# Equal groups of 64 rows, and no early store, in a two-way expert dispatch

## The chip, the cores and the metric

The kernel runs on one core of one Trainium2 chip. The metric is the device time in microseconds (us) of that core. Three runs of the kernel before took 239.65, 239.90 and 239.91 us, so the median is 239.9 us.

## The reference

There are 16 x 1024 = 16384 tokens. Each has a vector x of 512 floats and 8 router logits. The softmax of the logits gives eight probabilities, the two largest are kept and divided by their sum, and the token's vector is written out twice, once times each of the two weights:

```python
topk_indices = np.argsort(probs, axis=-1)[..., -k:]            # k = 2
topk_probs = np.take_along_axis(probs, topk_indices, axis=-1)
topk_probs = topk_probs / np.sum(topk_probs, axis=-1, keepdims=True)
x_expanded = x[:, :, np.newaxis, :].repeat(k, axis=2)
return (x_expanded * topk_probs[..., np.newaxis]).astype(np.float32)
```

The smaller of the two weights comes first. In bytes: x is 33.55 MB, the logits are 0.52 MB and the output is 67.11 MB.

## The kernel before, in words

**Layout.** Tokens are dealt to the 128 partitions of the on-chip memory in two groups. In a group of G rows, partition p holds G consecutive tokens; a "row" here is one token in each of the 128 partitions. A row of x is 2 KB in each partition (262,144 bytes in all) and a row of output is 4 KB in each partition (524,288 bytes). The groups have 65 and 63 rows (`GROUPS`, line 42), so in DRAM the pieces of two neighbouring partitions lie 65 or 63 times 2 KB apart in x, and 65 or 63 times 4 KB apart in the output.

**Buffers.** `xs` has room for 65 rows of x. `osp` has room for 18 rows of output, and its first two and a half rows also serve as scratch for the choice of the two largest logits. `WA` holds the two weights of every token.

**Weights.** `top2_weights` (lines 15 to 38) halves the eight logits three times with max and min on VectorE, takes the difference of the two largest and sends it through two sigmoids on ScalarE. Both groups' weights are made at once, after the logits have landed.

**Loads.** `LOADS` (line 44) gives the rows of each load: 6, 28 and 31 in the first group, 4, 28 and 31 in the second. They are issued on SyncE's DMA queue, with the two logits transfers (lines 144 and 145) behind the first. The 4-row load of the second group goes out on ScalarE's queue instead, behind a dummy activation (line 128, `pause`) that waits until the store ahead of the last one has landed. A load into rows of `xs` waits until the store that reads those rows has landed.

**Products and stores.** `STORES` (lines 47 to 50) lists each store: its first row, its number of rows, and where the products are put. "osp" means the buffer `osp` from the given row. "xs" means that the products overwrite rows of `xs` whose x is used up: the tensor-tensor product of line 164 makes 16 rows out of `xs` rows that it writes 32 rows of. Where rows of `osp` are used again, the product is cut in two (`FREE`, line 54): the rows that no store is reading come first, the rest waits until the earlier store has landed. In the first store of the second group, ScalarE makes the last 4 rows (`ACT_ROWS`, line 157), with two activations a row, and VectorE the other 12.

**Order.** Loads and stores are kept in program order on each queue. On SyncE's queue that is: load 6, logits, logits, load 28, load 31, the stores of 15, 16, 15 and 16 rows, load 28, load 31, and the stores of 16, 16, 15 and 16 rows. The first store of all, 3 rows, is issued on ScalarE's queue (line 175).

Of the kernel before, what the change touches and what calls it, by code (L numbers as in the profile page):

```python
# [1 line left out]

# [4 lines left out]

F32 = mybir.dt.float32
ALU = mybir.AluOpType
ACTF = mybir.ActivationFunctionType  # L10
P = 128


def top2_weights(nc, WA, dlt, room, logits, E):

    tt = nc.vector.tensor_tensor
    hi, lo, n = None, None, E  # L20
    while n > 1:
        n //= 2
        if hi is None:
            a, b = logits[:, :, 0:n], logits[:, :, n : 2 * n]
            nhi, nlo = room(n), b
            tt(nhi, a, b, op=ALU.max)  # L26
            tt(nlo, a, b, op=ALU.min)  # L27
        else:
            a, b = hi[:, :, 0:n], hi[:, :, n : 2 * n]
            nhi, nlo, tmp = room(n), room(n), room(n)  # L30
            tt(tmp, lo[:, :, 0:n], lo[:, :, n : 2 * n], op=ALU.max)  # L31
            tt(nlo, a, b, op=ALU.min)  # L32
            tt(nlo, nlo, tmp, op=ALU.max)  # L33
            tt(nhi, a, b, op=ALU.max)  # L34
        hi, lo = nhi, nlo
    tt(dlt, hi[:, :, 0], lo[:, :, 0], op=ALU.subtract)  # L36
    nc.scalar.activation(WA[:, :, 0], dlt, ACTF.Sigmoid, scale=-1.0)  # L37
    nc.scalar.activation(WA[:, :, 1], dlt, ACTF.Sigmoid, scale=1.0)  # L38

GROUPS = [65, 63]

LOADS = [[6, 28, 31], [4, 28, 31]]
BASE = [0, 1]

STORES = [
    [(0, 3, "osp", 0), (3, 15, "osp", 3), (18, 16, "xs", 0), (34, 15, "osp", 0), (49, 16, "xs", 33)],
    [(0, 16, "osp", 2), (16, 16, "xs", 0), (32, 15, "osp", 0), (47, 16, "xs", 32)],
]  # L50

L = 18

FREE = [3, 2]

ACT_ROWS = 4


@with_exitstack
def kernel(  # L60
    ctx: ExitStack,
    tc: tile.TileContext,
    x: bass.AP,
    router_logits: bass.AP,
    k: bass.AP,
    out: bass.AP,
):
    nc = tc.nc
    B, S, D = x.shape
    E = router_logits.shape[-1]  # L70
    N = B * S
    assert int(k) == 2 and E == 8 and N == P * sum(GROUPS)
    M = N // P

    x_v, o_v, rl_v = [], [], []
    t0 = 0
    for n in GROUPS:
        t1 = t0 + P * n
        x_v.append(
            x.rearrange("b s d -> (b s) d")[t0:t1].rearrange("(p m) d -> p m d", p=P)  # L80
        )
        o_v.append(
            out.rearrange("b s k d -> (b s) k d")[t0:t1].rearrange(
                "(p m) k d -> p m k d", p=P
            )
        )
        rl_v.append(
            router_logits.rearrange("b s e -> (b s) e")[t0:t1].rearrange(
                "(p m) e -> p m e", p=P
            )  # L90
        )
        t0 = t1

    wpool = ctx.enter_context(tc.tile_pool(name="wpool", bufs=1))
    xs = wpool.tile([P, max(GROUPS), D], F32)
    osp = wpool.tile([P, L, 2, D], F32)
    WA = wpool.tile([P, M, 2], F32)
    dlt = wpool.tile([P, M], F32)


    flat = osp.rearrange("p l k d -> p (l k d)")
    taken = [0]

    def room(n):
        o = taken[0]
        taken[0] += M * n
        return flat[:, o : o + M * n].rearrange("p (m n) -> p m n", n=n)

    logits = room(E)

    def place(where, at, n):

        if where == "osp":
            return osp[:, at : at + n]
        return xs[:, at : at + 2 * n, :].rearrange("p (r k) d -> p r k d", k=2)

    m0 = 0
    stores = []
    for g, G in enumerate(GROUPS):
        x0, r = BASE[g], 0  # L120
        for n in LOADS[g]:

            late = g == 1 and r == 0
            if late:


                rows = xs[:, x0 : x0 + 2, :]
                pause = nc.scalar.activation(rows, rows, ACTF.Copy)  # L128
                tc.add_manual_dep(
                    pause.ins,  # L130
                    stores[-2].ins.name,
                    mybir.DependencyInfo(
                        mybir.DependencyClass.Sync, mybir.DependencyReason.DATA
                    ),
                    reason="begin when the store ahead of the last has landed",
                )
                tc.keep_in_program_order(pause)
            queue = nc.scalar if late else nc.sync
            load = queue.dma_start(xs[:, x0 + r : x0 + r + n, :], x_v[g][:, r : r + n, :])  # L139
            tc.keep_in_program_order(load)  # L140
            r += n
            if g == 0 and r == 6:
                n0 = GROUPS[0]
                tc.keep_in_program_order(nc.sync.dma_start(logits[:, :n0], rl_v[0]))  # L144
                tc.keep_in_program_order(nc.sync.dma_start(logits[:, n0:], rl_v[1]))  # L145
                top2_weights(nc, WA, dlt, room, logits, E)
        assert r == G
        for r, n, where, at in STORES[g]:
            og = place(where, at, n)

            again = where == "osp" and at == 0 and r > 0
            cuts = [0, FREE[g], n] if again else [0, n]
            if g == 1 and r == 0:
                cuts = [0, n - ACT_ROWS]
                for j in range(n - ACT_ROWS, n):
                    for k2 in range(2):
                        nc.scalar.activation(  # L157
                            og[:, j, k2, :],
                            xs[:, x0 + r + j, :],
                            ACTF.Copy,  # L160
                            scale=WA[:, m0 + r + j, k2 : k2 + 1],
                        )
            for a, b in zip(cuts, cuts[1:]):
                nc.vector.tensor_tensor(  # L164
                    og[:, a:b],
                    xs[:, x0 + r + a : x0 + r + b, :]
                    .unsqueeze(2)
                    .to_broadcast([P, b - a, 2, D]),
                    WA[:, m0 + r + a : m0 + r + b, :]
                    .unsqueeze(3)  # L170
                    .to_broadcast([P, b - a, 2, D]),
                    op=ALU.mult,
                )

            queue = nc.scalar if g == r == 0 else nc.sync
            stores.append(queue.dma_start(o_v[g][:, r : r + n], og))  # L176
            tc.keep_in_program_order(stores[-1])
        m0 += G


# [1 line left out]
_INS = ['x', 'router_logits', 'k']  # L182
_OUTS = [((16, 1024, 2, 512), 'float32')]

_NUMBERS = {'k': 2}


# [26 lines left out]
```

## Time and profile before

| | |
|---|---|
| median of three runs | 239.9 us (239.65 to 239.91) |
| span of the profiled execution | 238.1 us |
| time outside that span, by the median | 1.8 us |
| VectorE busy | 137.6 us, 22 instructions |
| ScalarE busy | 7.9 us, 12 instructions |
| bytes moved by DMA | 101.19 MB, mean 425 GB/s over the span |
| time of the packets on the two DMA queues, as a share of 16 engines' span | 96.1% and 2.6% |

The page gives no time of its own for the profiled execution beside its span, so the median is set beside it. A transfer of 128 partitions is carried out by 16 DMA engines together. "To landing" is the time from the issue of a transfer to the semaphore that tells of its arrival, so it includes the time spent behind earlier transfers of its queue. In the chain of work, which is followed back from the last instruction, such a stretch of waiting is shown as one piece.

### The profile page before, as it was taken

What the parts mean: (1) busy time and instruction counts of PE and PEld (TensorE: products, weight loads), DVE (VectorE), ACT (ScalarE), POOL (GpSimd) and SP (SyncE); (2) the same over time, 40 slices, a digit from 0 to 9 for tenths busy, and PEclk for the clock granted to TensorE, in tenths of its full rate; (3) what the DMA queues carried; (4) which work ended last, traced back from release to release, by engine and by line L of the source; (5) the groups of instructions that cost most, each with busy time, mean ns of one, the idle gap of its engine ahead of it and who ended that gap; (6) DMA issues with size and microseconds to landing.
All of it is one profiled execution on the core that took longest, in us unless ns stands there. A gap on an engine that the chain in (4) does not pass through costs nothing.

```text
span 238.1 us, 115 instructions
## 1 busy us (share of the span) xinstructions
DVE 137.6 (58%) x22; ACT 7.9 (3%) x12; POOL 0.2 (0%) x4
## 2 busy tenths in 40 slices
DVE  0560499999789999100000009999936999950000
ACT  2000000000000000010000007000000000000000
POOL 0000000000000000000000000000000000000000
DMA  7979998979998999989999899898989989979894
GB/s 262 533 337 519 430 418 374 496 341 495 462 396 374 506 433 392 495 352 483 486 396 417 376 479 501 352 506 363 517 363 451 429 363 495 485 341 517 352 528 176
DMA packets 2448, 101.19 MB, mean 425 GB/s; under 512 B 272, under 2 KB 400, under 8 KB 528
## 3 DMA queue, kind: packets, MB, share of 16 engines
q1 hardware_dynamic: 2160, 98.57, 96.1%
q10 hardware_dynamic: 288, 2.62, 2.6%
HBM read 34.08 MB, written 67.11 MB: 425 GB/s over the span
## 4 chain that ended last, share of the span: by engine, by line
DMA 50%; DVE 38%; SPq 1%; issue 0%; DVEq 0%
DMA xs<-in_x_dram 30%; DVE osp L164 24%; DMA out_dram<-osp 20%; DVE xs L164 14%; SPq L144 0%; SPq L145 0%; SPq L139 0%; SPq L176 0%; DVEq L164 0%
## 5 line engine op out<-in xcount | busy, mean ns | idle before, releaser
L164 DVE TENSOR_TENSOR osp<-xs,WA 128x3072 f32<-128x3072 f32 (+4 forms) x7 | 65.1, 9298 | 65.6 <-DMA xs<-in_x_dram 56.8
L164 DVE TENSOR_TENSOR xs<-xs,WA 128x16384 f32<-128x16384 f32 x4 | 68.9, 17225 | 0.2
L157 ACT ACTIVATE osp<-xs,WA 128x512 f32<-128x512 f32 x8 | 5.0, 708 | 37.6 <-DMA xs<-in_x_dram 37.6
L26 DVE TENSOR_TENSOR osp<-osp 128x512 f32<-128x512 f32 x1 | 0.7, 692 | 8.4 <-DMA osp<-in_router_logits_dram 8.4
L128 ACT ACTIVATE xs<-xs 128x1024 f32<-128x1024 f32 x1 | 1.1, 1056 | 90.8 <-DMA out_dram<-osp 90.8
L37 ACT ACT_TABLE_LOAD x1 | 1.3, 1283 | 0.7 <-PEq L195 0.7
L27 DVE TENSOR_TENSOR osp<-osp 128x512 f32<-128x512 f32 x1 | 0.7, 691 | 0.0
L32 DVE TENSOR_TENSOR osp<-osp 128x256 f32<-128x256 f32 (+1 forms) x2 | 0.7, 350 | 0.0
L31 DVE TENSOR_TENSOR osp<-osp 128x256 f32<-128x256 f32 (+1 forms) x2 | 0.7, 350 | 0.0
L33 DVE TENSOR_TENSOR osp<-osp 128x256 f32<-128x256 f32 (+1 forms) x2 | 0.7, 350 | 0.0
L34 DVE TENSOR_TENSOR osp<-osp 128x256 f32<-128x256 f32 (+1 forms) x2 | 0.7, 348 | 0.0
L37 ACT ACTIVATE WA<-dlt 128x128 f32<-128x128 f32 x1 | 0.3, 317 | 10.3 <-DVE dlt L36 10.3
L36 DVE TENSOR_TENSOR dlt<-osp 128x128 f32<-128x128 f32 x1 | 0.3, 292 | 0.0
L38 ACT ACTIVATE WA<-dlt 128x128 f32<-128x128 f32 x1 | 0.3, 299 | 0.0
L195 POOL MEMSET const-bfloat16-1.0<- 128x1 bf16 x1 | 0.1, 102 | 0.0
L195 POOL MEMSET const-uint8-127<- 128x1 uint8 x1 | 0.1, 102 | 0.0
L195 POOL MEMSET const-float32-1.0<- 128x1 f32 x1 | 0.1, 99 | 0.0
L195 POOL MEMSET const-float32-0.0<- 128x1 f32 x1 | 0.1, 98 | 0.2 <-issue 0.2
## 6 DMA issues: line engine op xcount, KB each, us to landing
out_dram<-osp SPq DMA_DIRECT2D x3, 7680.0 KB, 23.4
xs<-in_x_dram SPq DMA_DIRECT2D x2, 7936.0 KB, 40.9
xs<-in_x_dram SPq DMA_DIRECT2D x2, 7168.0 KB, 35.2
xs<-in_x_dram SPq DMA_DIRECT2D x1, 1536.0 KB, 6.2
out_dram<-osp ACTq DMA_DIRECT2D x1, 1536.0 KB, 24.7
xs<-in_x_dram ACTq DMA_DIRECT2D x1, 1024.0 KB, 24.8
osp<-in_router_logits_dram SPq DMA_DIRECT2D x1, 260.0 KB, 6.4
osp<-in_router_logits_dram SPq DMA_DIRECT2D x1, 252.0 KB, 6.6
```

The source lines that it names most:

```text
L26: tt(nhi, a, b, op=ALU.max)
L27: tt(nlo, a, b, op=ALU.min)
L31: tt(tmp, lo[:, :, 0:n], lo[:, :, n : 2 * n], op=ALU.max)
L32: tt(nlo, a, b, op=ALU.min)
L33: tt(nlo, nlo, tmp, op=ALU.max)
L34: tt(nhi, a, b, op=ALU.max)
L36: tt(dlt, hi[:, :, 0], lo[:, :, 0], op=ALU.subtract)
L37: nc.scalar.activation(WA[:, :, 0], dlt, ACTF.Sigmoid, scale=-1.0)
L128: pause = nc.scalar.activation(rows, rows, ACTF.Copy)
L157: nc.scalar.activation(og[:, j, k2, :], xs[:, x0 + r + j, :], ACTF.Copy, scale=WA[:, m0 + r + j, k2 : k2 + 1],)
L164: nc.vector.tensor_tensor(og[:, a:b], xs[:, x0 + r + a : x0 + r + b, :] .unsqueeze(2) .to_broadcast([P, b - a, 2, D]), WA[:, m0 + r + a : ...
L195: nc = _bacc.Bacc("TRN2", target_bir_lowering=False, num_devices=1)
```

## The change

Both groups get 64 rows. The first group's three loads (6, 28, 31 rows) become two of 32 rows. The logits come in one transfer between these two, instead of in two behind the first load of 6 rows. The first group's five stores (3, 15, 16, 15, 16 rows) become four of 16, and the one of 3 rows that went out early on ScalarE's queue is no more: all stores are on SyncE's queue. The second group has four stores of 16 rows too (one had 15), and its last load has 32 rows instead of 31. ScalarE now takes part in the first store of both groups, with 5 rows in the first and 4 in the second. Where rows of `osp` are used again, 2 rows are free at once in both groups.

```diff
-GROUPS = [65, 63]
-
-LOADS = [[6, 28, 31], [4, 28, 31]]
-BASE = [0, 1]
+GROUPS = [64, 64]
+
+LOADS = [[32, 32], [4, 28, 32]]
+BASE = [0, 0]
 
 STORES = [
-    [(0, 3, "osp", 0), (3, 15, "osp", 3), (18, 16, "xs", 0), (34, 15, "osp", 0), (49, 16, "xs", 33)],
-    [(0, 16, "osp", 2), (16, 16, "xs", 0), (32, 15, "osp", 0), (47, 16, "xs", 32)],
+    [(0, 16, "osp", 2), (16, 16, "xs", 0), (32, 16, "osp", 0), (48, 16, "xs", 32)],
+    [(0, 16, "osp", 2), (16, 16, "xs", 0), (32, 16, "osp", 0), (48, 16, "xs", 32)],
 ]
 
-FREE = [3, 2]
-
-ACT_ROWS = 4
+FREE = [2, 2]
+
+ACT_ROWS = [5, 4]
...
-            if g == 0 and r == 6:
+            if g == 0 and r == 32:
                 n0 = GROUPS[0]
-                tc.keep_in_program_order(nc.sync.dma_start(logits[:, :n0], rl_v[0]))
-                tc.keep_in_program_order(nc.sync.dma_start(logits[:, n0:], rl_v[1]))
+                assert GROUPS[1] == n0
+                both = router_logits.rearrange("b s e -> (b s) e").rearrange(
+                    "(g p m) e -> p g (m e)", g=2, p=P
+                )
+                at = logits.rearrange("p (g m) e -> p g (m e)", g=2)
+                tc.keep_in_program_order(nc.sync.dma_start(at, both))
                 top2_weights(nc, WA, dlt, room, logits, E)
...
-            if g == 1 and r == 0:
-                cuts = [0, n - ACT_ROWS]
-                for j in range(n - ACT_ROWS, n):
+            if r == 0:
+                cuts = [0, n - ACT_ROWS[g]]
+                for j in range(n - ACT_ROWS[g], n):
...
-            queue = nc.scalar if g == r == 0 else nc.sync
-            stores.append(queue.dma_start(o_v[g][:, r : r + n], og))
+            stores.append(nc.sync.dma_start(o_v[g][:, r : r + n], og))
```

More of the change, by code (lines that the diff above doesn't have):

```diff
@@ L84 @@
                 "(p m) k d -> p m k d", p=P
[L85 to L89, printed above, removed]
             )
```

2 lines of the change are left out of this document (1 added, 1 removed).

## The prediction, made before the result was known

> **What bounds the kernel now.** I read the page first: which engine is busy, and how full the DMA is.
>
> ```profile
> span 238.1 us, 115 instructions
> DVE 137.6 (58%) x22; ACT 7.9 (3%) x12; POOL 0.2 (0%) x4
> DMA  7979998979998999989999899898989989979894
> DMA packets 2448, 101.19 MB, mean 425 GB/s; under 512 B 272, under 2 KB 400, under 8 KB 528
> q1 hardware_dynamic: 2160, 98.57, 96.1%
> q10 hardware_dynamic: 288, 2.62, 2.6%
> HBM read 34.08 MB, written 67.11 MB: 425 GB/s over the span
> ```
>
> The two queues' packets fill 96.1 + 2.6 = 98.7% of 16 engines' span, while VectorE is busy for 58% of it. The DMA engines are the bound, and no slice shows a hole. The change moves the same 101.19 MB. So the question is only what stands beside pure transfer: the start, the end, and stretches that run below the best rate.
>
> The second view is the chain of work in order of time (start, length, what):
>
> ```profile
> 0.73 0.38 SPq L139
> 2.11 24.91 DMA xs<-in_x_dram
> 27.04 16.17 DVE osp L164
> 43.23 22.90 DMA out_dram<-osp
> 66.15 12.97 DVE osp L164
> 79.14 17.24 DVE xs L164
> 96.78 45.47 DMA xs<-in_x_dram
> 142.37 12.97 DVE osp L164
> 155.40 25.13 DMA out_dram<-osp
> 180.55 14.04 DVE osp L164
> 194.61 17.23 DVE xs L164
> ```
>
> The products in it are links of semaphores, not the bound: the queue was full beside them. The useful thing is that each DMA piece ends with a landing: load 28 at 27.0, the 15-row store at 66.13, the second load 28 at 142.25, the next store at 180.53. Other landings come from the DMA view, asked for the stretch in which one transfer is issued. First the opening 48 us (size, us to landing), then the stores issued at 79.14 and 211.86:
>
> ```profile
> xs<-in_x_dram SPq DMA_DIRECT2D x1, 7936.0 KB, 45.3
> out_dram<-osp SPq DMA_DIRECT2D x1, 7680.0 KB, 22.9
> xs<-in_x_dram SPq DMA_DIRECT2D x1, 7168.0 KB, 24.9
> xs<-in_x_dram SPq DMA_DIRECT2D x1, 1536.0 KB, 6.2
> out_dram<-osp ACTq DMA_DIRECT2D x1, 1536.0 KB, 24.7
> osp<-in_router_logits_dram SPq DMA_DIRECT2D x1, 252.0 KB, 6.6
> ...
> out_dram<-osp SPq DMA_DIRECT2D x1, 7680.0 KB, 24.4
> ...
> out_dram<-xs SPq DMA_DIRECT2D x1, 25.4
> ```
>
> And the timeline, for issue times and product durations:
>
> ```profile
> 1.64 0.42 SPq L145 DMA_DIRECT2D osp<-in_router_logits_dram  x1
> 8.37 0.69 DVE L26 TENSOR_TENSOR osp<-osp 128x512 f32<-128x512 f32 x1 [8.37 <-DMA osp<-in_router_logits_dram]
> 12.84 3.36 DVE L164 TENSOR_TENSOR osp<-xs,WA 128x3072 f32<-128x3072 f32 x1 [0.58 <-ACT WA L38]
> 16.23 0.38 ACTq L176 DMA_DIRECT2D out_dram<-osp  x1
> 142.32 5.01 ACT L157 ACTIVATE osp<-xs,WA 128x512 f32<-128x512 f32 x8 [37.62 <-DMA xs<-in_x_dram]
> 180.55 14.02 DVE L164 TENSOR_TENSOR osp<-xs,WA 128x13312 f32<-128x13312 f32 x1 [5.71 <-DMA out_dram<-osp]
> 211.86 0.33 SPq L176 DMA_DIRECT2D out_dram<-xs  x1
> ```
>
> **Where the 238.1 us go.** A row of x is 0.262 MB, a row of output 0.524 MB. The best rate is that of the last three stores: 47 rows, 24.64 MB, between the landings at 180.53 and 211.86 + 25.4 = 237.26, that is 434.4 GB/s. All 101.19 MB at that rate take 232.9 us. The rest:
> - Start: the second logits transfer lands at 1.64 + 6.6 = 8.24. From the first issue at 0.73 that is 7.51 us for 2.10 MB, which need 4.83. So 2.68 us go to the first byte and the last landing.
> - First group, 8.24 to 66.13: 57.89 us for 59 rows of loads and 18 of stores, the early one among them: 24.90 MB, 57.32 us. Lost: 0.57 us.
> - Stores of 16 and 15 rows up to 79.14 + 24.4 = 103.54: 37.41 us for 16.25 MB, 37.42 needed. Nothing lost.
> - 103.54 to 142.25: a 16-row store, loads of 4 and 28 rows, 16.78 MB: 38.71 us for 38.62. Lost: 0.09.
> - 142.25 to 180.53: a 31-row load and a 16-row store, 16.51 MB: 38.28 for 38.02. Lost: 0.26.
> - End: 238.1 - 237.26 = 0.85 us.
>
> Sum: 0.73 + 2.68 + 232.9 + 0.57 + 0.09 + 0.26 + 0.85 = 238.1. The median stands 1.8 us above this span, and I take that as it is.
>
> **The change part by part.** Durations of the products first (mean ns, then idle before):
>
> ```profile
> L164 DVE TENSOR_TENSOR xs<-xs,WA 128x16384 f32<-128x16384 f32 x4 | 68.9, 17225 | 0.2
> L164 DVE TENSOR_TENSOR osp<-xs,WA 128x12288 f32<-128x12288 f32 x2 | 25.9, 12957 | 48.4 <-DMA xs<-in_x_dram 46.0 <-DMA out_dram<-osp 2.4
> L157 ACT ACTIVATE osp<-xs,WA 128x512 f32<-128x512 f32 x8 | 5.0, 708 | 37.6 <-DMA xs<-in_x_dram 37.6
> ```
>
> Sixteen rows take 17.23 us and twelve 12.96, so a row is 1.067 us. Twelve rows took the same with ScalarE at work beside them (142.37) as without (66.15).
>
> *Loads of 32 rows, logits between.* The first load and the logits are 8.91 MB: 20.52 us at the best rate, plus the start's 2.68, from 0.73: logits land at 23.9 instead of 8.24. The weights follow as before: from landing to the first product 12.84 - 8.24 = 4.6 us, so 28.5. VectorE makes 11 rows, 12.96 - 1.07 = 11.89 us, until 40.4. ScalarE's 5 rows, 10 activations at 5.01/8 = 0.63 us, end by 34.9 and are hidden. The first store is issued at 40.4 on SyncE, behind nothing that waits. The second load lands at 23.9 + 8.39 MB/434.4 = 43.2. This is the one cover that gets thin: the queue holds work for 2.8 us when the store is issued. How soon does an issue reach the engines? The DMA view between 1.6 and 2.1 has the first packets of the issue at 0.73 (packets, MB, share of 16 engines):
>
> ```profile
> q1 hardware_dynamic: 13, 0.16, 161.4%
> ```
>
> So packets flow 0.9 to 1.4 us after an issue, here by 41.8. The landing signal comes after the data, so the data may end up to half a microsecond ahead of 43.2. Cover left: about 1 us. Cost taken: nothing. Bounds: below, no gain, as there was no hole here before; above, a whole new start, 2.68 us, less the 1 us, is 1.7.
>
> Could the start itself be shorter? The first packets now carry 64 KB instead of 12 KB. The row above gives 161.4% of 16 x 0.5 us over 13 packets: 0.99 us each, against 0.45 at 434.4/16 GB/s. That is one slow first packet an engine, which a larger one would have too. Later small pieces run near the rate. Bounds 0 and -0.3; I take -0.1. One logits transfer instead of two takes 0.42 us off SyncE's queue at a time when the queue is full: nothing.
>
> *No early store.* Its 1.57 MB go out later with the rest, so its bytes cost the same. What goes is its interleaving with the loads on a second queue, between 16.23 and 40.9. The stretch that holds it lost 0.57 us over 59 rows of loads, while the loads of 32 rows beside a store on the other queue lost 0.09. If the first group now loses as that stretch did, 64 rows cost 0.18: -0.39. Bounds: all of the 0.57 goes; or the loss belongs to loads and is as in the 31-row stretch, 0.26/31 a row, which over 64 rows is 0.54, so it stays. I take -0.39, as the two well measured mixtures of load and store (0.09, and nothing at 66 to 103) say that neither loads nor stores must lose, and only this stretch had short pieces of a store among long pieces of a load.
>
> *Four stores of 16 rows.* VectorE's part behind the reuse of `osp` is 14 rows, 15.1 us, instead of 12 in the first group and 13 in the second. First group: store 1 lands at 43.2 + 19.3 = 62.5, the 14 rows end at 77.7, store 2 runs until 81.9: cover 4.2 us. The in-place product before it ends at 40.4 + 17.2 = 57.7, and store 1 covers it until 62.5. The fourth is ready at 94.9, store 3 runs to 101.2. Second group: all bytes ahead of load 28 are a row of loads and a row of stores fewer than before, 0.79 MB or 1.8 us, so it lands at 140.0 to 140.4; 12 rows as before, store 5 issued at 153.5 while the 32-row load runs until 159.8. Store 5 lands at 179.1, 14 rows to 194.2, store 6 until 198.4: cover 4.2 us. Nothing, with 4 us of room in each.
>
> *Pause and loads of the second group.* The pause on ScalarE still waits for store 3, now at 101.2; nothing is queued behind it there but the 4-row load and ScalarE's 8 products. On SyncE the 28-row load stands behind store 4 and has its rows free since store 2. Nothing.
>
> *The pitch.* Partitions' pieces in DRAM now lie exactly 128 KB apart in x and 256 KB in the output; before they were 2 KB or 4 KB off these. No row of before has this. Nearest rows: stores at 65 rows' pitch lost nothing, at 63 rows' pitch ran at the best rate. Below: loads stop losing even 0.26, -0.35 with the 0.09. Above: everything loses as the worst load did, 0.26 us on 18.7 us of load, 1.4%; on 232.9 us that is 3.3, less the 0.92 lost already: +2.3. I take nothing, by the stores, which are two thirds of the bytes and insensitive to 65 or 63. The Trainium skill speaks against the change here: DMA: Bandwidth & Descriptors, Latency and other measured facts, has copies with a per-partition pitch of 512 KiB at 207 GB/s and with larger powers of two as low as 103, where a padding of 4 KiB restores 214. By 207 against 214, an estimate from that page, 3.3% on all of the transfer would be 7.7 us. The pitches here are smaller than any it lists, and no trace here shows one.
>
> Sum: -0.39 - 0.1 = -0.49, so 239.9 - 0.5 = **239.4**. Its own range is 239.0 to 239.7.
>
> **The rivals.**
> *Nothing changes, 239.8.* The early store was hidden in a full queue anyway, and the 0.57 us are the loads' own. For it: the 31-row load lost 0.26 with no second queue active. Against: the 32 rows that lost 0.09. The first group then loses 0.54, the start may give 0.1.
> *Slower: the queue runs dry before store 1, 241.0.* Place: 42 to 44 us. Price: up to 1.7 us on 239.4, so 240.4 to 241.1. It decides if store 1 is issued after about 41.5, or if an engine must see the next transfer more than 2 us ahead to go on without a gap. For it: 2.8 us of queue is the least of all junctions, the next is 4. Against: packets flowed at most 1.4 us after an issue.
> *Slower: power-of-two pitch, 242.2.* By the upper bound above, +2.3. For it: loads do lose at times that nothing in the kernel explains. Against: the stores' even rate. The page named above is the rule that stands behind this one.
>
> **How the numbers follow.** A measurement of this kernel can tell about 0.2% from no change, 0.5 us, as its three runs lie within 0.26 us. Chances: forecast with its better half, at or beyond 0.2% faster, 0.38; nothing changes, the weaker half of the forecast with it, 0.30; dry queue 0.14; pitch 0.15; something not seen, slower, 0.03. Faster 0.38, same 0.30, slower 0.32. The range runs from 238.8 (all losses of 0.92 and some of the start go) to 241.3 (dry queue at its price, a weak form of the pitch); a full pitch loss is left out.
>
> **What would show it.** Right: logits land near 24, store 1 is issued near 40.4 and the 32-row load lands near 43.2; store 1 lands 19.3 us later; the DMA slices show no hole; the first group loses under 0.3 us against 434.4 GB/s. Wrong: store 1 lands later than 63 (dry queue), or 32 rows of load take clearly more than 19.3 us, or 16 rows of store do (pitch). The prediction fails most easily on the 1 us of cover, on the pitch, and on the 0.57 being the loads' own.

## The result, and the profile after

The changed kernel takes 240.6 us (median of 11 executions, 240.0 to 242.4), the kernel before 239.77 us (239.6 to 240.0) beside it. The ratio is 1.0049, 95% interval 1.0032 to 1.0066: slower by half a per cent, where 239.4 us, 0.2% faster, was forecast. The time lies inside the stated range, on its slower side. A second measurement on another occasion gave 241.3 us and a ratio of 1.0054 (1.0027 to 1.0081). Besides the slower median, the executions of the changed kernel lie much further apart: in the two measurements 15 of its 23 took over 240.5 us. The kernel before does that too, but seldom: in the measurements below 9 of 117 executions, the longest of 242.0 us.

The profiled execution took 240.23 us, so it is one of the quicker ones. Its page, and the chain of work in order of time (start, length, what):

```profile
span 238.4 us, 120 instructions
DVE 132.2 (55%) x21; ACT 14.0 (6%) x22; POOL 0.2 (0%) x4
DMA  9899898989899898989989799999899998989894
q1 hardware_dynamic: 2000, 100.14, 97.6%
q10 hardware_dynamic: 144, 1.05, 1.1%
...
1.15 22.67 DMA osp<-in_router_logits_dram
28.32 11.90 DVE osp L163
40.30 22.23 DMA out_dram<-osp
95.32 44.82 DMA xs<-in_x_dram
153.25 26.30 DMA out_dram<-osp
```

The queues are still full, 97.6 + 1.1 = 98.7% of the span. The logits land at 23.82, the first store is issued at 40.30 and lands at 62.53, all within 0.1 us of the prediction's times (23.9, 40.4, 62.5). For the sum of losses two more landings are needed: the third store, issued at 77.67, and the last, issued at 211.95:

```profile
77.67 0.33 SPq L174 DMA_DIRECT2D out_dram<-osp  x1
211.95 0.33 SPq L174 DMA_DIRECT2D out_dram<-xs  x1
...
out_dram<-osp SPq DMA_DIRECT2D x1, 23.4
...
out_dram<-xs SPq DMA_DIRECT2D x1, 25.5
```

Against the same 434.4 GB/s as in the prediction:

| stretch | before, lost us | after, lost us | from what in the trace of after |
|---|---|---|---|
| start, to the logits' landing | 2.68 | 2.58 | 23.82 - 0.72 = 23.10 us for 8.91 MB |
| rest of the first group, to the store ahead of its last | 0.57 | 0.0 | 23.82 to 101.07: 77.25 us for 33.55 MB |
| fourth store, loads of 4 and 28 rows | 0.09 | 0.45 | 101.07 to 95.32 + 44.82 = 140.14: 39.07 us for 16.78 MB |
| last load and the second group's first store | 0.26 | 0.79 | 140.14 to 179.55: 39.41 us for 16.78 MB |
| last three stores | 0 | 0.0 | 179.55 to 237.45: 57.90 us for 25.17 MB |
| end | 0.85 | 0.95 | 238.4 - 237.45 |

So the 0.57 us that the early store's stretch had lost did go, all of it. But 0.36 and 0.53 us came up in the two stretches from the fourth store to the second group's first, which the change hardly touches. Net +0.3 us in the span, as seen: 238.1 to 238.4. The rest of the difference of the medians lies in executions that were not profiled here.

A finer view of the same: the DMA view of a stretch exactly 1 us long in which the last 16 pieces of a load start, one on each engine. Its share of 16 engines' time is then the mean length of a piece, 100% for 1 us. Ahead of the first group's first store on SyncE's queue, in the kernel before (pieces of 62 KB, 1.02 MB in all, 44.8 to 45.8 us) and in the changed kernel (64 KB, 1.05 MB, 39.8 to 40.8):

```profile
q1 hardware_dynamic: 16, 1.02, 235.3%
```

```profile
q1 hardware_dynamic: 16, 1.05, 242.2%
```

At 434.4/16 GB/s a 62 KB piece needs 2.34 us and a 64 KB piece 2.41, so neither lost anything there. Ahead of the second group's first store (kernel before, 157.6 to 158.6; changed kernel, 156.1 to 157.1):

```profile
q1 hardware_dynamic: 16, 1.02, 249.2%
```

```profile
q1 hardware_dynamic: 16, 1.05, 306.7%
```

These last pieces of a load took 0.15 us too long before and 0.65 us too long after. The loss is not spread over the transfer: it sits in the pieces that are on their way when the engines turn from loads to stores. I call such a place a switch, the first group's the first switch and the second group's the second.

The 0.36 us came up at a turn the other way. The last 16 pieces of the fourth store, of 64 KB, are followed by the loads of the second group (kernel before, 118 to 119; changed kernel, 118.3 to 119.3), and they took 2.42 us before and 2.63 after, on average 0.21 too long:

```profile
q1 hardware_dynamic: 16, 1.05, 241.8%
```

```profile
q1 hardware_dynamic: 16, 1.05, 262.6%
```

In the kernel before, the early store's stretch has its loss in load pieces too. These are pieces of 56 KB, which need 2.11 us, and start in two windows of 0.9 us (17.7 to 18.6, ahead of the store's first pieces, and 23.1 to 24.0, among its pieces). 251.0% and 276.6% of 0.9 us are 2.26 and 2.49 us, 0.15 and 0.38 too long:

```profile
q1 hardware_dynamic: 16, 0.92, 251.0%
...
q1 hardware_dynamic: 16, 0.92, 276.6%
```

### The profile page after: what moved, and what is told of

It reads as the page before. It is cut to its first block, busy times and chain, and to the rows that moved or that the text cites. A ratio compares the mean times of both kernels' runs of the same rounds, so it can differ in the third digit from the quotient of the medians.

```text
span 238.4 us, 120 instructions
## 1 busy us (share of the span) xinstructions
DVE 132.2 (55%) x21; ACT 14.0 (6%) x22; POOL 0.2 (0%) x4
## 3 DMA queue, kind: packets, MB, share of 16 engines
q1 hardware_dynamic: 2000, 100.14, 97.6%
q10 hardware_dynamic: 144, 1.05, 1.1%
## 4 chain that ended last, share of the span: by engine, by line
DMA 49%; DVE 39%; issue 0%; SPq 0%; ACT 0%; DVEq 0%
DVE osp L163 23%; DMA out_dram<-osp 20%; DMA xs<-in_x_dram 19%; DVE xs L163 14%; DMA osp<-in_router_logits_dram 10%; DVE osp L26 0%; DVE osp L27 0%; DVE osp L33 0%; DVE osp L34 0%; DVE osp L32 0%; DVE osp L31 0%; SPq L134 0%; SPq L174 0%; ACT WA L38 0%; DVE dlt L36 0%
## 5 line engine op out<-in xcount | busy, mean ns | idle before, releaser
L163 DVE TENSOR_TENSOR osp<-xs,WA 128x2048 f32<-128x2048 f32 (+3 forms) x6 | 59.6, 9934 | 55.6 <-DMA xs<-in_x_dram 45.3
L156 ACT ACTIVATE osp<-xs,WA 128x512 f32<-128x512 f32 x18 | 11.2, 707 | 37.9 <-DMA xs<-in_x_dram 37.9
## 6 DMA issues: line engine op xcount, KB each, us to landing
xs<-in_x_dram SPq DMA_DIRECT2D x1, 7168.0 KB, 44.8
```

What stands on the lines that cost most here:

```text
L156: nc.scalar.activation(og[:, j, k2, :], xs[:, x0 + r + j, :], ACTF.Copy, scale=WA[:, m0 + r + j, k2 : k2 + 1],)
L163: nc.vector.tensor_tensor(og[:, a:b], xs[:, x0 + r + a : x0 + r + b, :] .unsqueeze(2) .to_broadcast([P, b - a, 2, D]), WA[:, m0 + r + a : ...
```

## The experiments

Times are medians, "beside" is the kernel before, measured together with them. One theory was the dry queue (the first store comes too late), one the pitch, one the early store itself.

### The changed kernel again, more of ScalarE, the old pitch, the old early store

```diff
 e1_again: the changed kernel
 e2_act7:  ACT_ROWS = [7, 4]
 e3_65_63: GROUPS = [65, 63]; LOADS = [[32, 33], [4, 28, 31]]; first group's stores 16, 16, 17, 16
 e4_64_early: LOADS = [[6, 28, 30], [4, 28, 32]]; first group's stores 3 (ScalarE's queue), 15, 16, 14, 16
```

> The changed kernel as it is, so that the others have it beside them on the same chip. Every theory expects about 240.6 us, and runs that scatter more widely (240.0 to 242.4 so far) than those of the kernel before (239.6 to 240.0). If it comes out at 239.8 here, the loss depends on the chip.

> The changed kernel with 7 rows instead of 5 for ScalarE in the first group's first store, so that this store is issued about 2.1 us earlier, near 38.2, with 5 us of load still queued. Theory 'dry queue' (in some executions the queue empties between the second load and the first store): 239.7 and a scatter of 0.4 us, as before. Theory 'pitch' (pieces 128 KB and 256 KB apart make transfers stall): unchanged, 240.6 with the wide scatter. Theory 'early store' (the early 3-row store or the small first load did good): unchanged too.

> The changed kernel with groups of 65 and 63 rows: loads of 32 and 33, then 4, 28 and 31; stores of 16, 16, 17, 16, then 16, 16, 15, 16; no early store, logits behind the first load in two pieces. Only the distance of the partitions' pieces in DRAM is as in the kernel before. Theory 'pitch': 239.7 or less, narrow scatter. Theories 'dry queue' and 'early store': 240.6, wide scatter.

> Groups of 64 rows with the early store restored: loads of 6, 28 and 30 rows in the first group with the logits (one transfer) behind the first, stores of 3 (ScalarE's queue), 15, 16, 14 and 16 rows. Theory 'early store': 239.8, narrow scatter. Theory 'pitch': 240.6 or more, wide scatter. Theory 'dry queue': 239.8, as the junction has its old cover.

| kernel | us | lowest, highest | ratio to beside (239.79 us), 95% |
|---|---|---|---|
| e1_again | 241.3 | 239.95, 242.8 | 1.0054 (1.0027 to 1.0081) |
| e2_act7 | 240.7 | 240.4, 241.5 | 1.0041 (1.0029 to 1.0052) |
| e3_65_63 | 242.5 | 240.1, 242.9 | 1.0098 (1.0066 to 1.0130) |
| e4_64_early | 240.1 | 239.9, 242.2 | 1.0025 (1.0004 to 1.0047) |

Issuing the first store 1.9 us earlier (38.40) made the executions agree much better, but at 240.7, not 239.7: the last load pieces of the first group now took 3.40 us instead of 2.42, in the same 1-us view (39.8 to 40.8):

```profile
q1 hardware_dynamic: 16, 1.05, 339.9%
```

So a store that stands ready behind the last load piece lengthens that piece by 1 us in this kernel. In the kernel before, with its early store, the store also stood ready (issued at 43.23, the last load pieces start from 44.8 on), and they were not lengthened. The old pitch alone did not help (242.5), against the pitch theory, though this run was not a clean test: a load of 33 rows has 66 KB in each partition, and its pieces were cut in two, of 33 KB each. The early store, put back at the new pitch, gave most of the loss back by the median, 240.1. Three of its 12 executions still took 241.5 to 242.2 us, so by the ratio, 1.0025 in place of 1.0054, it gave back about half.

### Where the edge of the queue is, and the weights earlier

```diff
 f1_act3: ACT_ROWS = [3, 4]
 h1_act4: ACT_ROWS = [4, 4]
 h2_act6: ACT_ROWS = [6, 4]
 f2_logits_first: the logits' transfer moved ahead of the first load of x
```

> The changed kernel with 3 rows instead of 5 for ScalarE in the first store: issued 2.1 us later, near 42.4, when the second load's data end near 42.8. Theory 'edge of the queue' (a store issued under 3 us before the loads end comes too late in some executions, as an issue needs longer to reach busy engines than idle ones): the queue now runs dry in every execution, a hole of 0.6 us or more at 43 to 45 in the trace, 241.5 to 243. Theory 'onset' (when the first store's pieces stand ready behind the last load's pieces, those pieces take longer, 3399 ns instead of 2418 in the run with 7 rows): no such wait, so 240.0 plus only the hole by issue time, 0.6 to 1.0 us, so 240.6 to 241, and little scatter.

> The changed kernel with 4 rows instead of 5 for ScalarE in the first store: issued near 41.35, so its pieces reach the engines near 42.35, just as the last load pieces end (42.35 to 42.76 in the changed kernel). Theory 'edge' (some executions hit a hole, some don't): between 240.0 and 242.0 from one execution to the next, or already near 241.9 in all, as with 3 rows. Theory 'onset' alone (a loss only where the store waits behind the last load piece): 240.0 to 240.3, little scatter.

> With 6 rows: issued near 39.2, reaching the engines near 40.2, while the last load pieces start (39.93 to 40.34). Theory 'edge': less scatter than with 5 rows, since there are 2 us of queue behind it. Theory 'onset': some engines have the store in view before their last load piece starts and lose about 1 us on it, others don't: 240.0 to 240.8, with scatter. With 7 rows it was 240.74, with 5 rows 241.26.

> The changed kernel with the logits ahead of the first load of x, so that the weights are there when the first load lands, and the first store is issued near 36, 7 us before the loads end. No early store. Theory 'edge of the queue': narrow scatter, 240.0 to 240.2 if nothing else is lost. Theory 'onset': narrow scatter, but the last pieces of the second load take about 1 us longer as in the run with 7 rows: 240.6 to 240.9. If it scatters up to 242 as the changed kernel does, both fall.

With the changed kernel's own 5 rows, a series by the time at which the first store is issued:

| kernel | first store issued at | us | lowest, highest |
|---|---|---|---|
| f2_logits_first | 35.8 | 241.0 | 240.8, 241.4 |
| e2_act7 | 38.4 | 240.7 | 240.4, 241.5 |
| h2_act6 | 39.5 | 240.8 | 240.6, 242.1 |
| e1_again | 40.4 | 241.3 | 239.95, 242.8 |
| h1_act4 | 41.3 | 240.9 | 240.6, 241.1 |
| f1_act3 | 42.5 | 241.9 | 241.9, 242.1 |

With 3 rows the queue runs dry, and it is seen: between 42.2 and 43.2 no load or store piece starts at all (the 16 records of no size are the signals of landing), and the store's 16 pieces start in the next microsecond.

```profile
42.52 0.35 SPq L174 DMA_DIRECT2D out_dram<-osp  x1
...
q1 hardware_dynamic: 16, 0.00, 0.9%
...
q1 hardware_dynamic: 16, 1.05, 245.5%
```

The issue at 42.52 reaches the engines in about a microsecond, just as the prediction had read it from the start of the kernel. In the changed kernel itself the same stretch, 42.2 to 43.2, has all 16 pieces of the store: no hole. With 4 rows, 1 us later than the changed kernel, there was still none. So the dry queue has its edge between 41.3 and 42.5, the changed kernel stands before it, and the dry queue is not what slowed it.

The other end is f2_logits_first. The store waits 7 us for its turn there, the executions agree within 0.6 us, and the last load pieces (39.8 to 40.8) are the longest of all, 3.57 us, 1.15 too long. Ahead of the second group's store (157.2 to 158.2) they take 2.71, 0.3 too long:

```profile
q1 hardware_dynamic: 16, 1.05, 356.7%
...
q1 hardware_dynamic: 16, 1.05, 270.8%
```

With 3 rows it is the other way round: nothing too long at the first switch (the hole put off the first store's landing by 0.8 us, 42.52 + 20.8 = 63.3 against 62.53 in the changed kernel), and 3.30 us, 0.88 too long, at the second (157.7 to 158.7):

```profile
q1 hardware_dynamic: 16, 1.05, 329.6%
```

With 4 rows no load piece was too long at the first switch either. The last pieces of the fourth store (119 to 120) took 2.91 us there, 0.50 too long, and the last load pieces at the second switch (156.7 to 157.7) 3.23, 0.81 too long:

```profile
q1 hardware_dynamic: 16, 1.05, 291.2%
...
q1 hardware_dynamic: 16, 1.05, 322.7%
```

No theory alone fits the series. 'Edge' had the 241.9 of 3 rows within its range, and missed with 7 rows (239.7 from the 'dry queue') and with 4 (wide scatter or 241.9). 'Onset' alone came within 0.1 us for f2_logits_first, and missed with 4 rows (240.0 to 240.3) and with 3 (241 at most). A store in good time pays about 1 us at the first switch, a store just in time pays nothing there and more at the later turns.

### Is it the piece, or the switch?

```diff
 f3_tail:        f2_logits_first with LOADS = [[32, 28, 4], [4, 28, 28, 4]]
 f4_before_tail: the kernel before with LOADS = [[6, 28, 31], [4, 28, 27, 4]]
 i3_last31:      the changed kernel with LOADS = [[32, 32], [4, 29, 31]]
```

> As the run with the logits first, and the last load of each group cut in two, 28 and 4 rows, so that the pieces just ahead of a store are of 8 KB instead of 64 KB. Theory 'onset' with a cost by piece (a last piece in flight takes longer by some share): most of the 1 us in the first group and the 0.4 us in the second go, 239.6 to 239.9. If the cost is a fixed time for the switch from loads to stores, 240.6 to 240.9 as without the cut.

> The kernel before with its last load cut into 27 and 4 rows. Its last load pieces ahead of the second group's stores took 0.15 us longer. Theory 'onset' by piece: 239.6 to 239.7. Fixed cost of the switch: 239.8, unchanged.

> The changed kernel with the second group's loads as 4, 29 and 31 rows, so that the pieces ahead of its first store are of 62 KB instead of 64 KB, at the same 64-row pitch. Theory 'piece of 64 KB' (0.65 and 0.41 us longer in the two traces of the changed kernel, against 0.15 in the kernel before): 0.0 to 0.2 us longer, 240.1 at best, 240.8 in the middle. Theory 'pitch' for this one switch: 0.4 to 0.65 us as before.

f3_tail took 240.9 us, as without the cut (241.0): with 8 KB pieces ahead of the store the switch costs about the same, so its price goes with the switch and not with the piece. The trace agrees. The 94 pieces of 8 KB that start between 40.3 and 43 took 0.46 us each (100.5% of 16 engines' 2.7 us), 0.16 more than the 0.30 they need, which is 0.9 us for each engine:

```profile
q1 hardware_dynamic: 94, 0.77, 100.5%
```

f4_before_tail took 239.94, ratio 0.9999 (0.9984 to 1.0014): no gain to be had there.

i3_last31 failed for its purpose, and was costly in a telling way: 242.6 us, ratio 1.0109 (1.0086 to 1.0131). A load of 29 rows behind the 4 reaches one row of `xs` that the fourth store reads, so the load waited for that store. The chain of work shows a load that begins only when a store has landed:

```profile
95.07 27.67 DMA out_dram<-xs
122.80 20.18 DMA xs<-in_x_dram
```

The engines were without work for 1.4 us there. It says nothing on 62 KB against 64 KB at the changed kernel's own timing; j1_65_63_even below has pieces of 62 KB that took 0.72 us too long.

### Smaller early store; no second queue

```diff
 h3_early1:         64-row groups; LOADS = [[6, 26, 32], ...]; stores of 1 (ScalarE's queue), 15, 16, 16, 16
 i1_no_side:        the changed kernel with LOADS[1] = [32, 32], both on SyncE's queue, no pause
 i2_before_no_side: the kernel before with LOADS[1] = [32, 31], both on SyncE's queue, no pause
```

> Groups of 64 with an early store of a single row (4 KB pieces) on ScalarE's queue, then stores of 15, 16, 16 and 16 rows; loads of 6, 26 and 32 rows, logits behind the 6. Theory 'the first write of the execution costs once, and is cheap if its pieces are small and lie between loads': 240.0, as with the early store of 3 rows and 64-row groups (240.08), and the last load pieces of the first group take no longer than 2418 ns. If the early store must be on its way until shortly before the main stores to help: the last pieces lose about 1 us again, 240.7 to 241.

> The changed kernel with the second group's loads as two of 32 rows on SyncE's queue: no 4-row load and no pause on ScalarE, so no second queue at all. Theory 'side load' (mixing two queues lets one engine fall behind, and the last landing waits for it): scatter of 0.4 us or less, near 240.1 to 240.4. Theory 'first junction' (engines part company between the second load and the first store): scatter stays, 240.0 to 242.5.

> The kernel before with the second group's loads as 32 and 31 rows on SyncE's queue, the early store kept. Theory 'side load': 239.7 to 239.9, no rare outliers above 240.2. Otherwise unchanged, 239.8, or slower if the mixture of the 4 rows with the store spares a longer switch from stores to loads: up to 240.5.

An early store of 1 row helped less than one of 3: 241.3 us, from 240.3 to 242.4, and the last load pieces at the first switch took 2.96 us (41.0 to 42.0), 0.54 too long, where those of e4_64_early took 2.31 (44.0 to 45.0; 60 KB, 2.26 needed):

```profile
q1 hardware_dynamic: 16, 1.05, 295.5%
```

```profile
q1 hardware_dynamic: 16, 0.98, 231.0%
```

So the early store of 3 rows spares the first switch its microsecond, and it isn't any early write that does so. (The two kernels also differ in their loads, and the main store was issued 0.5 us ahead of these pieces with 1 row, 1.2 us with 3.) The second switch was not spared: in e4_64_early the last load pieces there (156.4 to 157.4) took 0.43 us too long.

```profile
q1 hardware_dynamic: 16, 1.05, 284.5%
```

Taking the 4-row load off the second queue changed little: 240.7 us with the scatter still there (240.1 to 241.9, ratio 1.0036, 1.0021 to 1.0051), and for the kernel before 239.94, 1.0004 (0.9993 to 1.0015).

### Traces of slower executions

> The kernel with groups of 65 and 63 rows and no early store once more, for a trace of an execution at its usual 242.5 us (the trace so far is of one at 240.08). Theory 'edge': a hole or a longer last load piece at 41 to 46 us, and later losses at the second group's junctions. If the loss lies elsewhere in the trace, the junction isn't it.

> The changed kernel once more, for a trace. If this execution takes over 240.8: a single engine's landings trail the others' by 0.5 us or more from one of the three junctions on (first load to store near 42, side load 103 to 127, second load to store near 159), and the place tells which.

i4_again took 240.83 us. At the second group's switch (156.1 to 157.1) its last load pieces took 2.98 us on average. Then the store: 15 of its first 16 pieces start between 159.1 and 160.1, the sixteenth between 160.1 and 161.1 (each piece comes with one record of a landing signal here). At the end the same: 15 pieces of the last store start between 233.0 and 234.6, and one alone between 235 and 236.

```profile
q1 hardware_dynamic: 16, 1.05, 297.7%
...
q1 hardware_dynamic: 30, 0.98, 227.5%
q1 hardware_dynamic: 2, 0.07, 15.2%
...
q1 hardware_dynamic: 15, 0.98, 141.7%
q1 hardware_dynamic: 1, 0.07, 15.1%
```

In the quicker trace all 16 started by 160.1. At the switch the piece that started last (156.92) was also the longest, 3.56 us. The delay is not made good again: one piece is alone at the end too, and the last landing waits for it, as it would if each engine had a fixed share of every transfer. h4_65_63_again (242.3 us) shows the same with another cause: two engines were some 2.2 and 2.6 us behind the others after the 4-row load had been mixed with the fourth store, and the second load of 28 rows landed at 97.76 + 46.73 = 144.5 instead of 97.52 + 44.69 = 142.2 in the quicker trace of that kernel. At its end two pieces of 64 KB start between 235 and 237.5, when the other engines have none left to start (the other 14 records are signals of landing):

```profile
q1 hardware_dynamic: 16, 0.13, 12.4%
```

```profile
97.76 46.73 DMA xs<-in_x_dram
```

```profile
97.52 44.69 DMA xs<-in_x_dram
```

This is where the scatter comes from in these two slower executions. That all of them are of this kind is not shown.

### Pitch and early store, one at a time

```diff
 j1_65_63_even:      GROUPS = [65, 63]; LOADS = [[1, 32, 32], [4, 28, 31]]; first group's stores 16, 16, 15, 2, 16
 j2_before_no_early: the kernel before; first group's stores 16, 16, 15, 2, 16; FREE = [2, 2]; ACT_ROWS = [5, 4]
```

> The changed kernel's order with groups of 65 and 63 rows and no piece above 64 KB: loads of 1, 32 and 32 rows with the logits behind the second, stores of 16, 16, 15, 2 and 16 rows, then the second group of the kernel before. No early store, first store issued near 41, 3 us before the loads end. Theory 'pitch': the last load pieces ahead of the second group's stores take up to 0.4 us longer, no engine trails by 0.5 us, 239.8 to 240.1 with a scatter of 0.4 us. Theory 'early store': 240.6 and scatter, as with 64 rows.

> The kernel before without the early store: same loads (6, 28, 31 rows, logits behind the 6), stores of 16, 16, 15, 2 and 16 rows, 5 rows of the first on ScalarE; first store issued near 38, 6 us before the loads end. Theory 'pitch': the last load pieces of the first group take 0.1 to 0.4 us longer, 239.6 to 239.9, so the early store is worth nothing. Theory 'early store': they take 1 us longer, as they do with 64 rows and the logits first (1.15 us), and the time is 240.4 to 240.8.

j1_65_63_even took 240.6 us (240.1 to 242.7; 1.0038, 1.0014 to 1.0062): at the old pitch, without pieces over 64 KB, it is as slow and as scattered as the changed kernel. Its last load pieces took 2.42 us at the first switch (40.5 to 41.5), and 3.06 at the second (157.4 to 158.4), 0.72 too long. j2_before_no_early took 240.3 us (240.2 to 240.7). The median is 0.44 us over the kernel before (239.9), 0.18%; by the interval over all executions, 1.0008 (0.9990 to 1.0027), that is not clear of no change. Its trace shows the loss plainly: at the first switch (40.1 to 41.1) the 62 KB pieces took 3.48 us, 1.14 too long, and at the second (158.2 to 159.2) 2.34, nothing too long.

```profile
q1 hardware_dynamic: 16, 1.02, 306.2%
```

```profile
q1 hardware_dynamic: 16, 1.02, 348.4%
...
q1 hardware_dynamic: 16, 1.02, 234.2%
```

The three kernels with 65 and 63 rows, beside each other, in us too long at the switches: the kernel before 0.0 and 0.15, and in its early store's stretch about 0.5; j2_before_no_early 1.14 and 0; j1_65_63_even 0 and 0.72, and the last pieces of the fourth store 0.27. What one switch is spared, another pays. In sum the kernel before, with its early store, pays least.

## Why the prediction was wrong, step by step

- **The bound and the sum of the span** held: a full DMA queue before and after, and the difference is in the losses beside pure transfer.
- **Loads of 32 rows, logits between: nothing.** The times of this step came out within 0.1 us, and there was no hole. The cover of "about 1 us" was right too: 1 us later (4 rows) there was still no hole, 2.1 us later (3 rows) there was one. The rival of the dry queue falls for the changed kernel.
- **The start, -0.1:** it gave 0.10.
- **No early store, -0.39. This is the step that failed.** The stretch that held the early store did lose nothing any more, 0.57 us gained, even more than the 0.39 that I took. The error was to see the loss as the early store's own, a nuisance of mixing short pieces with long ones, and to leave the other stretches as they were: their 0.09 and 0.26 us were to stay, at no cost ("Pause and loads of the second group. Nothing"). They grew by 0.36 and 0.53 us in the profiled execution, more than the 0.57 gained. The kernel before without its early store (j2) paid 1.14 us at one switch in place of 0.5 + 0.15, and the early store put back at 64 rows (e4) brought 240.1. So I take the early store's loss as a turn from loads to stores, paid at a cheap place. That it is one and the same cost is argued from these sums, not shown. And not all of the growth comes from the missing early store: with it (e4) the second switch still cost 0.43 us, 0.28 more than in the kernel before.
- **Bounds of that step.** "All of the 0.57 goes" to "it stays" left out that a loss can move to another place and grow there. The trace of before had a hint, the 0.26 us in the stretch with the 31-row load, which holds such a switch; I read it as a property of loads.
- **The range** holds the measured time by luck: its slow end was drawn from the dry queue and a weak form of the pitch, and the queue did not run dry.
- **Four stores of 16 rows:** the covers held, no stall is seen at the first or third store.
- **The pitch** as a rival, 242.2, did not come: plain pieces of 64 KB took 2.42 us at the new pitch, as at the old. The old pitch without the early store (j1) is as slow as the changed kernel. At 64 rows with the early store (e4) 0.25% (0.04 to 0.47) is left, in which the pitch and a few sizes change together, so a part of up to that size is open. The second switch points to such a part: where the first had paid about 1 us, it cost 0.29 and 0.36 us with 64 rows (f2, e2) and nothing with 65 and 63 (j2). No run separates the pitch from the last pieces' size, 64 KB against 62. The 3.3% that the prediction estimated from the figure for a pitch of 512 KiB in the Trainium skill (DMA: Bandwidth & Descriptors, Latency and other measured facts) is far from anything seen here at 128 and 256 KB.
- **What no step covered** is the scatter. The span of the profiled execution grew by 0.3 us, the median by 0.83, so over half of the slowdown does not show in that execution. In the slower one that was traced (i4), an engine that lost more than the others stayed last to the end.

No run beat the kernel before: the two edits of it, the cut last load and the loads without a second queue, came out level with it.

## What to carry to other kernels

In a kernel bound by DMA with a full queue, don't only ask whether the queue stays full: look at the pieces on their way when the direction turns from loads to stores, and price each turn, for instance by the mean length of the last pieces. A small transfer that looks useless in such a kernel may be paying for a turn at a cheap place; before it is taken out, ask where the turn goes. And an unevenness among the engines at one place was not made good in the two traces above; it was paid at the end.

## What the runs showed that was not expected

A load piece of 64 KB that takes 2.42 us takes 3.4 to 3.6 us when the first store stands ready behind it (e2, f2; 3.48 for 62 KB in j2). With 8 KB pieces instead, the time of the kernel is about the same. A first store that arrives while the last load pieces are already on their way lengthens nothing there (2.42 us in the changed kernel), but the next turns then cost more: 0.65 to 0.88 us at the second group's (changed kernel, j1, h1, f1), against 0 to 0.36 where the first had paid 1 us (j2, f2, e2). The line between the two is not sharp: one quick execution of the changed kernel (e1, 156 to 157) paid only 0.41. Why one turn spares the next is not settled by these runs: I can say where the time goes, not what in the engines makes it so.
